# Experts of a routed feed-forward stage: part of the gate and up weights as plain float32, the output factors on other engines, and the split weights in another place of memory

## The chip, the cores and the metric

The kernel runs on one core of one Trainium2 chip. The metric is the device time of one execution in microseconds (us), as the median of several runs. Lower is better. Everything is float32 in memory, and the result has to agree with a float32 reference.

## What is computed

The reference is a network of two blocks. The first has dilated attention, gated scans and a gated linear recurrence in turn; the second has a hybrid mixer (pooling, a state space scan and a delta rule scan) and, at its end, a feed-forward stage of 16 experts in which each expert picks its own 128 tokens (16 experts, 1024 tokens, capacity factor 2). Cut to the part in question:

```python
def expert_choice_ffn(h, router_w, w_gate, w_up, w_down):
    ...
    gate, idx = lax.top_k(jnp.swapaxes(aff, 1, 2), cap)
    xe = jax.vmap(lambda hb, ib: hb[ib])(h, idx)
    hid = jax.nn.silu(jnp.einsum('becd,edf->becf', xe, w_gate)) * jnp.einsum('becd,edf->becf', xe, w_up)
    ye = jnp.einsum('becf,efd->becd', hid, w_down) * gate[..., None].astype(h.dtype)
    return jax.vmap(lambda ib, yb: jnp.zeros((T, D), yb.dtype).at[ib.reshape(-1)].add(yb.reshape(-1, D)))(idx, ye)
...
        x = x + m_lat[5][:, None] * expert_choice_ffn(h_lat, router_w[l], exp_w_gate[l], exp_w_up[l], exp_w_down[l])
...
    return rms_norm(x, final_norm_g)
```

The model's width is D = 1024 and an expert's width is 512, so the three weights of an expert are 1024x512, 1024x512 and 512x1024: 6.3 MB as float32, and 100 MB for all 16.

## The kernel before, in words

The program is one long list of instructions for each engine, put in order ahead of time by a scheduler from the way the code is written, its priorities and its buffers; on the chip each engine takes its list strictly in order and waits on semaphores. Everything up to the choice of tokens is the same list on every engine before and after the change. What concerns us is the last part, the function `experts` (from L2009), some 410 us of the span, and the pools that are laid out for it in `second_end` (L2206 to L2227).

**Products in three parts.** TensorE multiplies float32 data in the faster format float32r, which keeps fewer bits. To keep the accuracy, each operand is split into a high part (a cast to float32r, on ScalarE) and a low part (the difference, on VectorE or GpSimd). `mm3` (L135 to L141) then issues three matmuls into the same PSUM bank: high by high (L139), high by low of the moving operand (L140), low by high (L141). In the traces the stationary operand is the tokens (xeh, xel), and the moving operand is the weights (ehi, elo).

**Weights.** `units` (L2015 to L2029) brings one weight matrix in four units of 128x1024 float32 (512 KB). For each it issues one transfer on SP (SyncE, L2022) into a buffer `eraw` (27 of them, 14 in one pool and 13 in a second), the cast `ehi` on ScalarE (L2023) and the subtraction `elo`: on VectorE (L2025) for units 0 to 2 of each matrix, on GpSimd (L2027) for the fourth, and for all units of expert 0 on GpSimd. There are four buffers of ehi and four of elo. A unit holds two 128-row slices of gate or up (k = 0 to 7), or one of down.

**One expert.** `gather(e)` (L2031) turns the choice into indices and fetches the 128 chosen rows `xe` by an indirect transfer that GpSimd issues (L2047). `hidden(e)` (L2054) transposes xe on TensorE in two PSUM tiles of four chunks (L2061), splits them into xeh and xel (L132, L133), and computes gate and up (24 matmuls of 128x512 each) in the PSUM banks called `a`; then tanh on ScalarE (L2073) and two VectorE instructions (L2074, L2075) make `hid`. `down(e)` (L2078) transposes hid, splits it (hidh, hidl) and multiplies by down into the two banks called `o`, 24 more matmuls. VectorE reads each half from PSUM, multiplies it by the token's gate and by the row m5 (L2092), and GpSimd adds the result `ye` to the tokens' rows in memory with an indirect transfer (`accd`, L2094). Experts 14 and 15 aren't scattered: their part is added by matmuls at the end.

**Order.** The loop (L2128) asks in one step for gather(e+1), hidden(e) and down(e-1), so that an expert's gate and up lie beside the down product of the expert before. The scheduler mixes the instructions of both. SP's list is nothing but the weight transfers, each waiting for a free buffer; GpSimd's list mixes elo, xe and accd, and an instruction that waits holds up all that is behind it.

**Memory.** The split weights are in the pool `ew` (L2212) at the right (upper) end of memory, and the second pool of raw buffers, `er2`, next to it.

Of the kernel before, what the change touches and what calls it, by code (L numbers as in the profile page):

```python
# [10 lines left out]
F32 = mybir.dt.float32  # L11
F32R = mybir.dt.float32r
U32 = mybir.dt.uint32
AF = mybir.ActivationFunctionType
ALU = mybir.AluOpType
# [4 lines left out]
P = 128  # L20
# [7 lines left out]
def dap(ap, dims, off=0):  # L28

    return bass.AP(tensor=ap.tensor, offset=ap.offset + off, ap=[list(d) for d in dims])  # L30
# [1978 lines left out]
def experts(g, pool, rps, wp, vals, iota, place, m5, h2d, accd, finish):  # L2009


    nc, I = g.nc, g.I
    turns = cycle(rps)

    def units(blk, e, k, n):  # L2015
        out = []
        for u in range(4):
            rp, bufs = next(turns)
            raw = rp.tile([P, 1024], F32, name="eraw", tag="eraw", bufs=bufs)
            hi = wp.tile([P, 1024], F32R, name="ehi", tag="ehi", bufs=4)  # L2020
            lo = wp.tile([P, 1024], F32R, name="elo", tag="elo", bufs=4)
            nc.sync.dma_start(raw.rearrange("p (k n) -> p k n", n=n), blk[:, u * k:(u + 1) * k, :])  # L2022
            nc.scalar.copy(hi, raw)  # L2023
            if u < 3 and e > 0 or e == 15:
                nc.vector.tensor_sub(lo, raw, hi.bitcast(F32))  # L2025
            else:
                nc.gpsimd.tensor_tensor(lo, raw, hi.bitcast(F32), op=ALU.subtract)  # L2027
            out += [(hi[:, i * n:(i + 1) * n], lo[:, i * n:(i + 1) * n]) for i in range(k)]
        return out  # L2029

    def gather(e):  # L2031

        oh = pool.tile([P, 8, P], BF16, name="onehot", tag="onehot", bufs=1)
        nc.vector.tensor_tensor(oh, iota[:, None, 0:P].to_broadcast([P, 8, P]),
                                place[:, e, :, None].to_broadcast([P, 8, P]), op=ALU.is_equal)
        ps = g.psum("tr")
        for i in range(8):
            nc.tensor.matmul(ps[:, :5], oh[:, i], vals[:, i, e], start=i == 0, stop=i == 7)
        pk = pool.tile([P, 5], F32, name="picked", tag="picked", bufs=2)
        with g.up():  # L2040
            nc.vector.tensor_copy(pk, ps[:, :5])
        fi = pool.tile([P, 2], F32, name="fi", tag="fi", bufs=2)
        nc.vector.scalar_tensor_tensor(fi[:, 0:1], pk[:, 0:1], 128.0, pk[:, 1:2], op0=ALU.mult, op1=ALU.add)
        idx = pool.tile([P, 1], U32, name="idx", tag="idx", bufs=5)
        nc.vector.tensor_copy(idx, fi[:, 0:1])
        xe = pool.tile([P, D], F32, name="xe", tag="xe", bufs=2)
        nc.gpsimd.indirect_dma_start(out=xe, out_offset=None, in_=h2d, in_offset=bass.IndirectOffsetOnAxis(ap=idx, axis=0),  # L2047
                                     bounds_check=T - 1)
        nc.vector.tensor_add(fi[:, 1:2], pk[:, 2:3], pk[:, 3:4])
        gate = pool.tile([P, 1], F32, name="gate", tag="gate", bufs=5)  # L2050
        nc.vector.tensor_add(gate, fi[:, 1:2], pk[:, 4:5])
        return xe, idx, gate, fi[:, 0:1]

    def hidden(e, xe):  # L2054

        xh = pool.tile([P, 8, P], F32R, name="xeh", tag="xeh", bufs=2)
        xl = pool.tile([P, 8, P], F32R, name="xel", tag="xel", bufs=2)
        for c0 in range(0, 8, 4):
            tr = g.psum("tr")
            for i in range(4):  # L2060
                nc.tensor.transpose(tr[:, i * P:(i + 1) * P], xe[:, (c0 + i) * P:(c0 + i + 1) * P], g.ident)  # L2061
            with g.up():
                g.split(xh[:, c0:c0 + 4], xl[:, c0:c0 + 4], tr.rearrange("p (c t) -> p c t", t=P))
        sta = [(xh[:, k], xl[:, k]) for k in range(8)]
        wg = units(I["we_gate"][e], e, 2, 512)
        pg = g.psum("a")
        g.mm3(pg, sta, wg)
        wu = units(I["we_up"][e], e, 2, 512)
        pu = g.psum("a")
        g.mm3(pu, sta, wu)  # L2070
        hid = pool.tile([P, 512], F32, name="hid", tag="hid", bufs=2)
        with g.up():
            nc.scalar.activation(hid, pg, AF.Tanh, scale=0.5)  # L2073
            nc.vector.scalar_tensor_tensor(hid, hid, 1.0, pg, op0=ALU.add, op1=ALU.mult)  # L2074
            nc.vector.scalar_tensor_tensor(hid, hid, 0.5, pu, op0=ALU.mult, op1=ALU.mult)  # L2075
        return hid

    def down(e, hid, idx, gate, place):  # L2078
        tr = g.psum("tr")
        for i in range(4):  # L2080
            nc.tensor.transpose(tr[:, i * P:(i + 1) * P], hid[:, i * P:(i + 1) * P], g.ident)
        hh = pool.tile([P, 4, P], F32R, name="hidh", tag="hidh", bufs=2)
        hl = pool.tile([P, 4, P], F32R, name="hidl", tag="hidl", bufs=2)
        with g.up():
            g.split(hh, hl, tr.rearrange("p (c t) -> p c t", t=P))
        wd = units(I["we_down"][e], e, 1, 1024)
        y = pool.tile([P, D], F32, name="ye", tag="ye", bufs=2)
        for half in range(2):
            hs = slice(half * 512, (half + 1) * 512)
            pd = g.psum("o")  # L2090
            g.mm3(pd, [(hh[:, k], hl[:, k]) for k in range(4)], [(h[:, hs], l[:, hs]) for h, l in wd])
            nc.vector.scalar_tensor_tensor(y[:, hs], pd, gate, m5[:, hs], op0=ALU.mult, op1=ALU.mult)  # L2092
        if e < 14:
            nc.gpsimd.indirect_dma_start(out=accd, out_offset=bass.IndirectOffsetOnAxis(ap=idx, axis=0), in_=y,  # L2094
                                         in_offset=None, bounds_check=T - 1, compute_op=ALU.add)
            return

        oh = pool.tile([P, T], F32R, name="oht", tag="xeh", bufs=2)
        nc.vector.tensor_scalar(oh, iota, place, None, op0=ALU.is_equal)
        if e == 14:  # L2100
            yh, yl = (pool.tile([P, D], F32R, name=nm, tag="xel", bufs=2) for nm in ("yh", "yl"))
        else:
            yh, yl = (wp.tile([P, D], F32R, name=nm, tag=nm, bufs=4) for nm in ("ehi", "elo"))
        for half in range(2):
            hs = slice(half * 512, (half + 1) * 512)
            g.split(yh[:, hs], yl[:, hs], y[:, hs])
        ends.append((oh, yh, yl))
        if e == 14:
            return
        rp, bufs = rps[0]  # L2110
        acc = []
        for tok in range(8):
            acc.append(rp.tile([P, D], F32, name="acc", tag="eraw", bufs=bufs))
            nc.sync.dma_start(acc[-1], accd[tok * P:(tok + 1) * P])
        for tok in range(8):
            for half in range(2):
                hs = slice(half * 512, (half + 1) * 512)
                ps = g.psum("mm")
                for i, (oh, yh, yl) in enumerate(ends):
                    nc.tensor.matmul(ps, oh[:, tok * P:(tok + 1) * P], yh[:, hs], start=i == 0, stop=False)  # L2120
                    nc.tensor.matmul(ps, oh[:, tok * P:(tok + 1) * P], yl[:, hs], start=False, stop=i == 1)
                with g.up():
                    nc.vector.tensor_add(acc[tok][:, hs], acc[tok][:, hs], ps)
            finish(acc[tok], tok)

    ends = []
    at = {0: gather(0)}
    for e in range(17):  # L2128
        if e < 15:
            at[e + 1] = gather(e + 1)  # L2130
        if e < 16:
            hid = hidden(e, at[e][0])
        if e > 0:
            down(e - 1, prev, *at[e - 1][1:])
        prev = hid


def second_end(g, mix, mods, out, close, banks):

    nc, I, tc = g.nc, g.I, g.tc  # L2140
    h2d = g.dram.tile([T, D], F32, name="h2d")
    accd = g.dram.tile([T, D], F32, name="accd")
    with ExitStack() as es:
# [65 lines left out]
        m5, g3 = ev.tile([P, D], F32, name="m5"), ev.tile([P, D], F32, name="g3")  # L2209
        nc.sync.dma_start(m5, dap(mods, [[0, P], [1, D]], 5 * D))  # L2210
        nc.sync.dma_start(g3, dap(I["norm3"], [[0, P], [1, D]]))
        wp = es.enter_context(g.pool("ew", "right"))  # L2212
        rq = es.enter_context(g.pool("er2", "right"))
        with g.pool("ch") as cp:
            nc.vector.tensor_copy(place, choose(g, cp, aff, consts))
# [12 lines left out]
def body(g, out):  # L2228
# [101 lines left out]
    def banks():  # L2330
        pe.close()
        pe.enter_context(g.psum_pool("ps3", mm=2, a=2, o=2, tr=2))
    second_end(g, mix, mods, out, close, banks)
    pe.close()

# [120 lines left out]
```

## Time and profile before

| what | value |
|---|---|
| median of 3 runs | 3650.38 us (3646.48 to 3652.74) |
| the profiled execution's own time | 3659.12 us |
| its span, first to last instruction | 3656.9 us |
| mean granted TensorE clock | 0.935 |
| busy share: TensorE matmul, VectorE, ScalarE, GpSimd | 88%, 70%, 44%, 39% |
| first gate matmul of expert 0, from the span's start | 3246.85 us |
| ye of expert 0, of expert 14, of expert 15 begins | 3300.59, 3617.75, 3624.60 us |

The profile shows one execution. PE is TensorE, PEld its weight loads, DVE is VectorE, ACT is ScalarE, POOL is GpSimd, SP is SyncE, which issues transfers; a name with q (SPq) is the engine's own instruction queue. The profiled execution took 8.7 us more than the median of the runs, 0.24%. In what follows places are told in us from the start of the span.

### The profile page before, as it was taken

The numbers are of one execution on the slowest core, as the hardware profiler recorded it, in microseconds if no ns is written. First come the engines' busy times: TensorE is split into PE (matmuls) and PEld (weight loads), VectorE is DVE, ScalarE is ACT, GpSimd is POOL, SyncE is SP. The second block draws the span as 40 slices with busy tenths as digits, with TensorE's granted clock in tenths as the row PEclk, the third lists the DMA queues.
The fourth block names the chain that finished last, engine by engine and source line by source line (L and its number), as shares of the span: only waits on it lengthen the run. The fifth ranks groups of instructions, "written<-read, shape, count | busy, mean of one in ns | idle before, by whom it ended". The sixth has DMA issues, their size and how long they took to land.

```text
span 3656.9 us, 63623 instructions
## 1 busy us (share of the span) xinstructions
PE 3228.8 (88%) x23752; PEld 2610.4 (71%) x23752; DVE 2576.0 (70%) x5604; ACT 1595.0 (44%) x3332; POOL 1439.0 (39%) x1431
## 2 busy tenths in 40 slices
PE   7998898999979999999999989688896878858887
PEld 6887776766658787878787867566675766636665
DVE  4776664346675777976868686779994765678887
ACT  3444434544324545455545441344433331235665
POOL 4657773000041333433334321723214563345553
PEclk9999999999989999999999999789997888969999
DMA  5223244253242211111112135234337655768994
GB/s 181 82 87 102 87 140 137 74 177 99 96 153 73 70 64 53 58 54 40 56 45 76 54 126 174 77 82 133 104 108 187 140 135 205 211 219 295 312 332 148
DMA packets 374001, 461.28 MB, mean 126 GB/s; under 512 B 150419, under 2 KB 280723, under 8 KB 373692
## 3 DMA queue, kind: packets, MB, share of 16 engines
q1 hardware_dynamic: 359852, 407.93, 36.1%
q0 software_dynamic: 13840, 49.29, 4.4%
q8 instruction: 187, 3.06, 0.4%
q14 instruction: 122, 1.00, 0.1%
HBM read 357.57 MB, written 104.27 MB: 126 GB/s over the span
## 4 chain that ended last, share of the span: by engine, by line
PE 46%; DVE 23%; DMA 9%; issue 9%; POOL 8%; ACT 3%; SPq 2%; DVEq 0%; POOLq 0%; ACTq 0%
PE mm L139 9%; PE mm L140 9%; PE mm L141 9%; PE a L249 2%; POOL aw L966 2%; DVE cacc L1145 2%; DVE elo L2025 2%; DMA srow<-rdsl 1%; DMA aw<-in_ada_w_dram 1%; PE a L406 1%; PE o L225 1%; POOL wlo L116 1%; DVE gtmp L1465 1%; PE a L141 1%; DVE u_kb L187 1%
## 5 line engine op out<-in xcount | busy, mean ns | idle before, releaser
L116 POOL TENSOR_TENSOR wlo<-wraw,whi 128x1024 fp32r<-128x1024 f32 (+1 forms) x131 | 328.2, 2509 | 528.1 <-ACT whi L115 517.7
L2023 ACT CAST ehi<-eraw 128x1024 fp32r<-128x1024 f32 x192 | 200.4, 1050 | 144.5 <-PE a L141 100.7
L139 PE MATMUL mm<-x1h,whi 128*128 128x512 f32 x576 | 235.4, 409 | 3.3 <-DVE G L921 1.7
L140 PE MATMUL mm<-x1l,whi 128*128 128x512 f32 x576 | 233.9, 406 | 1.8 <-DVE x1l L133 1.8
L141 PE MATMUL mm<-x1h,wlo 128*128 128x512 f32 x576 | 233.8, 406 | 0.0
L139 PE MATMUL mm<-whi,x1h 128*128 128x256 f32 x768 | 221.8, 289 | 0.4 <-DVE G L921 0.4
L2025 DVE TENSOR_TENSOR elo<-eraw,ehi 128x1024 fp32r<-128x1024 f32 x138 | 196.8, 1460 | 35.7 <-ACT ehi L2023 34.2
L141 PE MATMUL mm<-whi,x1l 128*128 128x256 f32 x768 | 219.6, 286 | 0.0
L140 PE MATMUL mm<-wlo,x1h 128*128 128x256 f32 x768 | 219.1, 286 | 0.0
L115 ACT CAST whi<-wraw 128x1024 fp32r<-128x1024 f32 (+1 forms) x131 | 136.0, 1040 | 158.0 <-PE mm L140 78.5
L2027 POOL TENSOR_TENSOR elo<-eraw,ehi 128x1024 fp32r<-128x1024 f32 x54 | 138.9, 2577 | 161.9 <-ACT ehi L2023 144.1
L140 PE MATMUL mm<-wlo,xh 128*128 128x256 f32 x640 | 185.5, 290 | 1.9 <-POOL wlo L116 1.9
L141 PE MATMUL mm<-whi,xl 128*128 128x256 f32 x640 | 185.5, 290 | 0.0
L139 PE MATMUL mm<-whi,xh 128*128 128x256 f32 x640 | 184.8, 290 | 0.0
L139 PE MATMUL mm<-x2h,whi 128*128 128x512 f32 x400 | 168.2, 420 | 10.2 <-ACT cu L1134 5.7
L139 PE MATMUL mm<-whi,yin 128*128 128x512 f32 x352 | 150.2, 430 | 23.4 <-DVE z L824 14.1
L141 PE MATMUL mm<-x2h,wlo 128*128 128x512 f32 x400 | 164.9, 413 | 0.8 <-POOL wlo L116 0.8
L140 PE MATMUL mm<-x2l,whi 128*128 128x512 f32 x400 | 164.9, 412 | 0.0
L966 POOL TENSOR_SCALAR aw<-aw,ac 128x128 f32<-128x128 f32 x256 | 123.7, 498 | 85.5 <-DMA aw<-in_ada_w_dram 51.9
L139 PE MATMUL mm<-xh,whi 128*128 128x512 f32 x336 | 137.6, 410 | 20.0 <-ACT whi L115 16.7
L139 PEld LDWEIGHTS mm<-whi,x1h 128*128 128x128 f32 x768 | 146.8, 191 | 3.1 <-issue 1.0
L140 PEld LDWEIGHTS mm<-wlo,x1h 128*128 128x128 f32 x768 | 146.8, 191 | 0.6
(742 smaller groups left out, 10437.4 us busy)
## 6 DMA issues: line engine op xcount, KB each, us to landing
eraw<-in_we_gate_dram SPq DMA_DIRECT2D x64, 512.0 KB
eraw<-in_we_up_dram SPq DMA_DIRECT2D x64, 512.0 KB
eraw<-in_we_down_dram SPq DMA_DIRECT2D x64, 512.0 KB
yin<-yd POOLq DMA_DIRECT2D x29, 1024.0 KB, 9.7
aw<-in_ada_w_dram SPq DMA_DIRECT2D x96, 256.0 KB
yd<-y_hl SPq DMA_DIRECT2D x80, 256.0 KB
wraw<-in_w_dram SPq DMA_DIRECT2D x25, 512.0 KB
wraw<-in_w_out_dram SPq DMA_DIRECT2D x24, 512.0 KB
```

Of the source, the lines that this page charges most:

```text
L115: nc.scalar.copy(hi[:, :sz], raw[:, :sz])
L116: nc.gpsimd.tensor_tensor(lo[:, :sz], raw[:, :sz], hi[:, :sz].bitcast(F32), op=ALU.subtract)
L139: nc.tensor.matmul(ps, sh, mh, start=first and i == 0, stop=False)
L140: nc.tensor.matmul(ps, sh, ml, start=False, stop=False)
L141: nc.tensor.matmul(ps, sl, mh, start=False, stop=last and i == n - 1)
L187: nc.vector.tensor_sub(c32(kb), bc[:, :, il:il + 1].to_broadcast([P, nck, 32]), bc)
L249: nc.tensor.matmul(ap[32 * c:32 * c + 32, o + lo:o + hi], sta[:, o + 32 * c:o + 32 * c + 32], mov[:, o + lo:o + hi], start=True, stop=True)
L966: nc.gpsimd.tensor_scalar(w[:, k], w[:, k], at(k), 0.0, op0=ALU.mult, op1=ALU.add)
L1145: nc.vector.scalar_tensor_tensor(acc, u[:, i:i + n], cw[:, i:i + 1], acc, op0=ALU.mult, op1=ALU.add)
L2023: nc.scalar.copy(hi, raw)
L2025: nc.vector.tensor_sub(lo, raw, hi.bitcast(F32))
L2027: nc.gpsimd.tensor_tensor(lo, raw, hi.bitcast(F32), op=ALU.subtract)
```

## The change

It does three things, in `experts` and its pools.

1. `units` has a new argument `plain`. Gate and up are called with plain=1: their fourth unit (k = 6 and 7) stays as it arrived, with no ehi and no elo. A new helper `product` does the first six slices by `mm3` and the last two with one ordinary float32 matmul each. For these, the last two of the eight chunks of the transposed tokens are copied as float32 (`xew`, by ScalarE), and xeh and xel are made for six chunks, so that the second half of each is 128x256 now.
2. For experts 0 to 13 ScalarE reads each half of the down product from PSUM and multiplies it by the gate; GpSimd then multiplies the whole 128x1024 tile by m5, ahead of the indirect transfer accd. Experts 14 and 15 keep the VectorE instruction.
3. The pool `ew` moves to the lower end of memory, above the tiles m5 and g3; `er2` takes its place at the upper end.

```diff
-    def units(blk, e, k, n):
+    def units(blk, e, k, n, plain=0):
+
         out = []
         for u in range(4):
             rp, bufs = next(turns)
             raw = rp.tile([P, 1024], F32, name="eraw", tag="eraw", bufs=bufs)
+            nc.sync.dma_start(raw.rearrange("p (k n) -> p k n", n=n), blk[:, u * k:(u + 1) * k, :])
+            if u >= 4 - plain:
+                out += [raw[:, i * n:(i + 1) * n] for i in range(k)]
+                continue
             hi = wp.tile([P, 1024], F32R, name="ehi", tag="ehi", bufs=4)
             lo = wp.tile([P, 1024], F32R, name="elo", tag="elo", bufs=4)
-            nc.sync.dma_start(raw.rearrange("p (k n) -> p k n", n=n), blk[:, u * k:(u + 1) * k, :])
             nc.scalar.copy(hi, raw)
...
+    def product(ps, sta, mov):
+
+        whole = [i for i, m in enumerate(mov) if not isinstance(m, tuple)]
+        parts = [i for i, m in enumerate(mov) if isinstance(m, tuple)]
+        g.mm3(ps, [sta[i] for i in parts], [mov[i] for i in parts], last=False)
+        for i in whole:
+            nc.tensor.matmul(ps, sta[i], mov[i], start=False, stop=i == whole[-1])
...
+        xw = pool.tile([P, 2, P], F32, name="xew", tag="xew", bufs=2)
...
+            t3 = tr.rearrange("p (c t) -> p c t", t=P)
+            m = min(4, 6 - c0)
             with g.up():
-                g.split(xh[:, c0:c0 + 4], xl[:, c0:c0 + 4], tr.rearrange("p (c t) -> p c t", t=P))
-        sta = [(xh[:, k], xl[:, k]) for k in range(8)]
-        wg = units(I["we_gate"][e], e, 2, 512)
+                g.split(xh[:, c0:c0 + m], xl[:, c0:c0 + m], t3[:, :m])
+                if c0 == 4:
+                    nc.scalar.copy(xw, t3[:, 2:4])
+        sta = [(xh[:, k], xl[:, k]) for k in range(6)] + [xw[:, k] for k in range(2)]
+        wg = units(I["we_gate"][e], e, 2, 512, 1)
         pg = g.psum("a")
-        g.mm3(pg, sta, wg)
-        wu = units(I["we_up"][e], e, 2, 512)
+        product(pg, sta, wg)
+        wu = units(I["we_up"][e], e, 2, 512, 1)
         pu = g.psum("a")
-        g.mm3(pu, sta, wu)
+        product(pu, sta, wu)
...
-            nc.vector.scalar_tensor_tensor(y[:, hs], pd, gate, m5[:, hs], op0=ALU.mult, op1=ALU.mult)
+            if e < 14:
+                nc.scalar.activation(y[:, hs], pd, AF.Copy, scale=gate)
+            else:
+                nc.vector.scalar_tensor_tensor(y[:, hs], pd, gate, m5[:, hs], op0=ALU.mult, op1=ALU.mult)
         if e < 14:
+            nc.gpsimd.tensor_tensor(y, y, m5, op=ALU.mult)
             nc.gpsimd.indirect_dma_start(out=accd, out_offset=bass.IndirectOffsetOnAxis(ap=idx, axis=0), in_=y,
...
-        wp = es.enter_context(g.pool("ew", "right"))
+        wp = es.enter_context(g.pool("ew"))
```

The scheduler makes a new order from this. Three places of it follow. In the rows the number is the instruction's line (lines of the changed file are some 4 to 18 higher), and "x3" means three alike behind each other.

GpSimd's list in the middle of the experts, about two experts of it, before:

```order
L2047 DMA xe<-h2d,idx 128x1024
L2027 TENSOR_TENSOR elo<-eraw,ehi 128x1024 x3
L2094 DMA accd<-ye,idx 1024x1024
L2047 DMA xe<-h2d,idx 128x1024
L2027 TENSOR_TENSOR elo<-eraw,ehi 128x1024 x3
L2094 DMA accd<-ye,idx 1024x1024
```

and now:

```order
L2114 TENSOR_TENSOR ye<-ye,m_33798 128x1024
L2115 DMA accd<-ye,idx 1024x1024
L2059 DMA xe<-h2d,idx 128x1024
L2031 TENSOR_TENSOR elo<-eraw,ehi 128x1024
L2114 TENSOR_TENSOR ye<-ye,m_33798 128x1024
L2115 DMA accd<-ye,idx 1024x1024
L2059 DMA xe<-h2d,idx 128x1024
L2031 TENSOR_TENSOR elo<-eraw,ehi 128x1024
```

Of the three subtractions of an expert one is left, that of down's fourth unit, and the multiplication by m5 stands new ahead of accd; xe and the subtraction stand behind both.

VectorE's list around an expert's ye, before:

```order
L133 TENSOR_TENSOR hidl<-tr,hidh 128x512
L2043 SCALAR_TENSOR_TENSOR fi<-picked 128x1
L2049 TENSOR_TENSOR fi<-picked 128x1
L2092 SCALAR_TENSOR_TENSOR ye<-o,gate,m_33798 128x512 x2
L2051 TENSOR_TENSOR gate<-fi,picked 128x1
L2025 TENSOR_TENSOR elo<-eraw,ehi 128x1024 x3
L2045 CAST idx<-fi 128x1
L2074 SCALAR_TENSOR_TENSOR hid<-hid,a 128x512
L2025 TENSOR_TENSOR elo<-eraw,ehi 128x1024 x3
L133 TENSOR_TENSOR xel<-tr,xeh 128x512 x2
```

and the same place now:

```order
L2029 TENSOR_TENSOR elo<-eraw,ehi 128x1024 x2
L2057 CAST idx<-fi 128x1
L2063 TENSOR_TENSOR gate<-fi,picked 128x1
L2029 TENSOR_TENSOR elo<-eraw,ehi 128x1024
L2091 SCALAR_TENSOR_TENSOR hid<-hid,a 128x512
L133 TENSOR_TENSOR xel<-tr,xeh 128x512
L133 TENSOR_TENSOR xel<-tr,xeh 128x256
L2029 TENSOR_TENSOR elo<-eraw,ehi 128x1024 x2
```

The two ye instructions are gone from VectorE, the second xel is half as large, and the xel pair stands ahead of more of the subtractions.

ScalarE's list of one expert now (before, it held no ye, and twelve ehi to an expert):

```order
L2027 CAST ehi<-eraw 128x1024 x4
L132 CAST xeh<-tr 128x512
L2027 CAST ehi<-eraw 128x1024 x2
L132 CAST xeh<-tr 128x256
L2110 ACTIVATE ye<-o,gate 128x512 x2
L2027 CAST ehi<-eraw 128x1024 x2
L132 CAST hidh<-tr 128x512
L2080 COPY xew<-tr 128x256
L2027 CAST ehi<-eraw 128x1024 x3
L2090 ACTIVATE hid<-a 128x512
```

The two ye stand ahead of casts of the next units, so that these wait until the down product is done.

## Rows read from the trace of the kernel before

**Rows 1.** PE's waits, 3240:3657: who waited for whom, us in total, times, longest.

```profile
PE a L140 <- POOL elo L2027: 15.7, 4, 5.8
PE a L140 <- DVE elo L2025: 14.1, 8, 4.7
PE a L141 <- DVE xel L133: 11.9, 7, 3.2
PE o L140 <- DVE elo L2025: 4.6, 6, 2.5
```

**Rows 2.** DVE's timeline at ye of experts 0, 1, 5, 14: start, duration.

```profile
3300.59 0.75 DVE L2092 SCALAR_TENSOR_TENSOR ye<-o,gate,m 128x512 f32<-128x512 f32 x1 [0.47 <-PE o L141]
...
3321.47 0.74 DVE L2092 SCALAR_TENSOR_TENSOR ye<-o,gate,m 128x512 f32<-128x512 f32 x1
...
3423.47 0.74 DVE L2092 SCALAR_TENSOR_TENSOR ye<-o,gate,m 128x512 f32<-128x512 f32 x1
...
3617.75 0.73 DVE L2092 SCALAR_TENSOR_TENSOR ye<-o,gate,m 128x512 f32<-128x512 f32 x1
```

**Rows 3.** Windows: length, busy us per engine (instructions), PEclk, DMA share, GB/s.

```profile
3369.00:3396.00 27.00, 21.34 (x94) 16.22 (x94) 19.42 (x23) 14.67 (x17) 16.94 (x6) 0.87 0.85 279
...
3465.00:3487.00 22.00, 19.21 (x94) 14.64 (x93) 20.23 (x24) 14.44 (x16) 8.73 (x5) 1.00 0.96 364
```

**Rows 4.** PE's timeline after its three kinds of long waits: start, duration, [idle before].

```profile
3264.03 0.79 PE L140 MATMUL a<-elo,xeh 128*128 128x512 f32 x1 [4.73 <-DVE elo L2025]
...
3292.56 0.80 PE L140 MATMUL a<-elo,xeh 128*128 128x512 f32 x1 [4.04 <-DVE elo L2025]
...
3411.87 0.80 PE L140 MATMUL a<-elo,xeh 128*128 128x512 f32 x1 [5.83 <-POOL elo L2027]
```

**Rows 5.** POOL's timeline, experts 5 (three rows) and 9 (last row).

```profile
3400.05 4.71 POOL L2094 DMA_INDIRECT accd<-ye,idx  x1 [1.69 <-DVE gate L2051]
3405.06 4.38 POOL L2047 DMA_INDIRECT xe<-h2d,idx  x1 [0.30 <-issue]
3409.46 2.36 POOL L2027 TENSOR_TENSOR elo<-eraw,ehi 128x1024 fp32r<-128x1024 f32 x1
...
3508.26 1.59 POOL L2094 DMA_INDIRECT accd<-ye,idx  x1 [0.16 <-issue]
```

**Rows 6.** DVE's timeline at four places.

```profile
3258.78 6.33 DVE L2025 TENSOR_TENSOR elo<-eraw,ehi 128x1024 fp32r<-128x1024 f32 x2
...
3405.02 3.48 DVE L2025 TENSOR_TENSOR elo<-eraw,ehi 128x1024 fp32r<-128x1024 f32 x3
...
3501.06 4.82 DVE L2025 TENSOR_TENSOR elo<-eraw,ehi 128x1024 fp32r<-128x1024 f32 x3 [0.21 <-ACT ehi L2023]
3505.80 1.40 DVE L2092 SCALAR_TENSOR_TENSOR ye<-o,gate,m 128x512 f32<-128x512 f32 x2
```

**Rows 7.** PE's timeline: float32 matmuls (L1153) among float32r ones; transposes.

```profile
2434.24 1.88 PE L1153 MATMUL tr<-cu,blockones 128*128 128x512 f32 x4
2435.56 0.80 PE L141 MATMUL mm<-x2h,wlo 128*128 128x512 f32 x1
2436.19 0.39 PE L139 MATMUL mm<-x2h,whi 128*128 128x512 f32 x1
...
2445.79 0.39 PE L141 MATMUL mm<-x2h,wlo 128*128 128x512 f32 x1
...
3503.75 1.03 PE L2061 MATMUL tr<-ident,xe 128*128 128x128 f32 x8
```

**Rows 8.** Prices: lines by form in 3300:3600; L2223 (ns min/median/max).

```profile
L2073 ACT ACTIVATE hid<-a 128x512 f32<-128x512 f32 x13 | 7.8, 598 | 7.7 <-PE a L141 6.7 <-PE a L140 1.0
...
L2223 POOL TENSOR_TENSOR acc<-acc,g x3: 2351/2408/2421, 3636.0 to 3646.7; 128x1024 f32<-128x1024 f32 x3
```

**Rows 9.** SP's waits before a weight transfer, 3080:3657: us, times, longest.

```profile
SPq L2022 <- DVE elo L2025: 132.9, 89, 6.9
...
SPq L2022 <- DMA eraw<-in_we_gate_dram: 7.9, 8, 1.4
```

## The prediction

> **What bounds the kernel now.** Only the experts change, so I read that stage alone, from its first gate matmul at 3246.85 us. First the waits of PE, since PE's list is the longest there. It waits 15.7 us for a POOL elo (4 times), 14.1 and 4.6 us for DVE elos and 11.9 us for xel [rows 1]. The POOL elo waits stand in front of matmuls into `a`, that is gate and up. The reader is to see that PE doesn't lack weights: it lacks their low halves.
>
> Then the pace, from one ye to the next [rows 2]. Expert 0 to 1 took 20.9 us, experts 1 to 5 (3423.47 - 3321.47)/4 = 25.5 us each, experts 5 to 14 (3617.75 - 3423.47)/9 = 21.6 us each. PE's own work sets the floor: 42 rows of float32r matmuls from 2436.19 to 2445.79 give 9.60/41 = 0.234 us each, and eight transposes take 1.03 us [rows 7]. An expert has 72 such matmuls and 12 transposes: 16.8 + 1.55 = 18.4 us. So the early experts lose 7 us each and the later ones 3.2.
>
> Then why they lose it. Early: POOL's list is in order. Its accd took 4.71 us, its xe 4.38 and only then came the elo (2.36) for which PE had idled 5.83 us [rows 4, 5]. Later, accd took 1.59 [rows 5]. After such an idle stretch PE runs below full clock: the window of one early expert has a granted clock of 0.87, a later one 1.00 [rows 3]. As the lower level is half, 0.87 means that some 7 of the 27 us ran at half clock, which cost up to 3.5 us beside the wait. Right at the start DVE was held instead: two elos took 6.33 us at 3258.78 where three in a row take 3.48 elsewhere, with POOL elos beside them, and PE idled 4.73 and 4.04 us [rows 4, 6]. Later it is xel: two ye (1.40 us) stand ahead of it on DVE [rows 6].
>
> **The change, part by part.**
>
> *Float32 quarter on PE.* Each of gate and up loses 6 float32r matmuls and gets 2 float32 ones. In the trace four L1153 instructions, which are two such matmuls of the program, and one float32r matmul take from 2434.24 to 2436.19, 1.95 us; less 0.234 that is 0.86 us for each float32 matmul of 128x512 [rows 7]. Per k: 0.86 instead of 0.70; per expert 4 x 0.16 = +0.64 us, on PE, so on the path: new floor 60 x 0.234 + 4 x 0.86 + 1.55 = 19.0 us. The bounds are 0.70 (no cost) and, at half clock, twice 0.86. The Trainium skill (FP8 and Floating Point Precision, TensorE Precision Notes) says that true float32 makes four passes through the array; by that a k would cost 4 x 0.234 = 0.94 us, by an estimate, and the 16 experts 4 x 0.08 x 16 = 5 us more than by the row, on which the sum goes.
>
> *Subtractions and casts dropped.* Two of POOL's three elos per expert go (2.36 each), exactly those of gate's and up's fourth units. So the wait that costs most has nothing left to wait for: k = 6 and 7 need only the raw weights, which are there long before. SP mostly waits for buffers (132.9 us for DVE elos alone) and rarely for a landing (7.9 us, 8 times) [rows 9]. ACT loses two casts and DVE half of one xel, off the path.
>
> *ye.* DVE loses 1.40 us per expert [rows 6], ahead of xel. ACT gets two reads of PSUM, not seen before in this form: the nearest row is tanh on 128x512 from PSUM, 0.598 us [rows 8]; ACT was busy 14.4 of 22 us [rows 3], so this and the xew copy (at most the same 0.6) hide. POOL gets a 128x1024 product of two tiles: L2223 took 2.41 (2.35 to 2.42) [rows 8]. POOL still ends 2 x 2.36 - 2.4 = 2.3 us lighter. But two kinds of instruction exclude each other: three DVE elos at 3501.06 took 4.82 us rather than 3.48, beside one POOL elo [rows 6]. The new product would do to a DVE elo what each POOL elo did: up to 2.4 us a time, once, where two such meetings go. I count the balance as nothing. The Trainium skill (SBUF — State Buffer, the two separate sides) calls it an exclusive lock between GpSimd and a DVE instruction with two SBUF inputs; the trace agrees, with the 4.82.
>
> *New waits.* On ACT, ye waits for the last matmul of down, and the casts behind it wait too. They are of the next units, with four buffers of each half, so up to four units of about 1.4 us of PE are in hand. On POOL, the product, accd, xe and down's fourth elo now stand behind ye: 2.4 + 4.7 + 4.4 + 2.4 = 13.9 us at the early, slow prices, against some 17 from ye to the point where the next down product needs that elo (a pace of 20.8 less two thirds of down's 24 x 0.234 us). 3 us in hand.
>
> *Memory places.* Split weights and raw buffers change places; all earlier owners are done long before, as the first weights land well ahead of use. Zero; below a few us late at the start if not, once.
>
> **The sum.** Against the profiled execution's 3659.1.
> - Before ye of expert 0: the 4.73 and 4.04 us go, with POOL relieved of two of 12 elos there, and about 2.5 us at half clock behind each (as 3.5 us in the early window): -14, less 2 x 0.64 of float32 cost: -13. Bounds: -6 if one stall stays, -19.
> - Experts 1 to 5, four paces: from 25.5 to the floor 19.0 plus what remains of the late loss. That loss is 3.2 us, of which 1.4 is ye ahead of xel: 19.0 + 1.8 = 20.8. So 4 x 4.7 = -19.
> - Experts 5 to 14, nine paces: 21.6 to 20.8: -7.
> - Expert 0 to 1 was 20.9 already: 0. Expert 15 and the end: the order there is alike; 0 to -3.
> Sum: -40, with ends worked out below. So the profiled execution would be 3619, and as it stood 8.7 us above the median of the runs shown, the median 3650.4 - 40 = 3610. I take **3609**, with 1 us of the end's bound. Cross-check from the waits [rows 1]: the POOL and DVE elo waits and xel sum to 46 us; if a third stays, 31 us go, and half clock of some 3 us on each of seven early experts gives 21 more; less 16 x 0.64 = 10: -42.
>
> **How far it can go.** Best: all 14 paces at 19.0 (they took 317 us): -51, and -13 ahead: 3586. Least, if the mechanism holds at all: only the 15.7 us and four half-clock stretches of 2.5 go, less 10: -16, 3635.
>
> **Rivals.**
> 1. *Only the early stalls go.* In the later experts the window of 22 us moves 364 GB/s at a DMA share of 0.96 [rows 3]. An expert's 26.4 us at 279 GB/s is 7.4 MB, and a pace of 20.8 needs 354 GB/s: hardly below that. For it: the share. Against it: SP waits for buffers, not landings [rows 9]. Then later paces stay at 21.6 or, with the float32 cost, 22.2: -13 - 4 x 3.6 + 0 to 5 = -22 to -27, so 3623 to 3628; chance 0.2.
> 2. *POOL's list becomes the bound* (slower). If accd and xe, at 4.7 and 4.4, are held 3 us longer than now, by DVE elos as they were in [rows 5], the elo of down comes too late in each expert: a stall as the 5.83 us one, and some 2.4 at half clock: 19.0 + 8.2 = 27.2 a pace rather than 22.65 on the mean of 14: +64, less the first 13: +51, 3701. It decides when ye-to-elo passes 17 us. For it: it adds 2.4 us ahead of accd. Against: POOL holds less work in all. Chance 0.04.
> 3. *Nothing to measure*: the stall moves from POOL's elo to DVE's (14.1 us already [rows 1]), because DVE and POOL exclude each other over the product as over the elos: early paces of 24.5, later ones 22: -4 + 4 - 5, 3645; chance 0.05.
>
> **How the numbers follow.** The forecast, 3609, has 0.7, with its own range 3594 to 3623. Rival 1 has 0.2, rival 3 has 0.05, rival 2 has 0.04; the last 0.01 is for anything slower. The range for 8 in 10 leaves out the best end and the last two rivals and takes in rival 1: 3592 to 3632. A measurement tells about 0.2%, 7 us. Faster by more: 0.7 + 0.2 + 0.02 of rival 3 = 0.92; within: 0.03; slower: 0.05.
>
> **What would show it.** In the changed profile: PE waits for POOL elo in front of `a` gone; ye of expert 0 (now on ACT) near 3288, paces near 20.8 from the first, granted clock near 1.00 in all windows; float32 matmuls of two instructions, 0.86 us; xel waits shorter; accd behind a POOL product of 2.4 us. Wrong if PE waits at `o` for a POOL elo, if ACT's ye holds casts so that PE waits for ehi, if the early accd and xe still stop PE, or if SP shows long waits for landings and later paces stay over 21.6.

## The result, and the profile after

The changed kernel takes 3603.97 us in the median of 4 runs (3598.18 to 3608.20), the kernel before 3650.98 (4 runs): the ratio is 0.9877, with a 95% interval of 0.9858 to 0.9896, so 47 us less by the medians and 45 by the ratio. The forecast was 3609. The profiled execution took 3603.50 us, its span is 3601.4 us, and the mean granted clock rose from 0.935 in the profiled execution of before to 0.943.

Of the 55.5 us between the two spans 5 are not the change's: the first transposes of expert 0 begin at 3240.02 us here and at 3245.06 before, and up to there the orders are the same. They begin anywhere from 3236 to 3245 in the traces of this case, and at 3240.62 in that of a kernel whose lists in the stage are those of before (part 3 alone, below). So I compare the *stage*, from those transposes to the end of the span: 411.8 us before, 361.4 after, 50 less. The two windows (columns as in [rows 3]), first before, then after:

```profile
3245.06:3656.90 411.84, 342.95 (x1520) 262.87 (x1520) 332.07 (x360) 243.84 (x276) 209.99 (x97) 0.93 0.79 263
...
3240.02:3601.40 361.38, 332.95 (x1456) 240.73 (x1456) 282.62 (x330) 226.19 (x288) 156.15 (x81) 0.96 0.84 300
```

PE was idle for 68.9 us of the stage before and for 28.4 after, 40.5 less. The rise of the granted clock from 0.93 to 0.96 is worth some 15 us more, by an estimate from these two rounded values. Against it stand some 10 us for the float32 matmuls. That makes some 45 of the 50 us.

PE's waits in the changed kernel, 3240:3602 (who waited for whom, us in total, times, longest), the counterpart of [rows 1]:

```profile
PE a L139 <- ACT xeh L132: 6.8, 4, 1.9
PE tr L2074 <- DMA xe<-h2d,idx: 5.7, 1, 5.7
PE a L140 <- DVE elo L2029: 4.8, 4, 2.1
...
PE a L141 <- DVE xel L133: 1.1, 1, 1.1
...
PE o L140 <- POOL elo L2031: 0.2, 1, 0.2
```

No wait for a POOL elo is left in front of gate and up (15.7 us in [rows 1]); those for DVE elos fell from 18.7 to 4.8 and those for xel from 11.9 to 1.1. The 5.7 us for the first xe were there before too.

The starts of ye for experts 0, 1, 5 and 9 on ACT and of expert 14 on DVE, from the timelines of the changed kernel, as in [rows 2]:

```profile
3275.17 1.27 ACT L2110 ACTIVATE ye<-o,gate 128x512 f32<-128x512 f32 x2
...
3294.72 1.27 ACT L2110 ACTIVATE ye<-o,gate 128x512 f32<-128x512 f32 x2
...
3373.27 1.26 ACT L2110 ACTIVATE ye<-o,gate 128x512 f32<-128x512 f32 x2
...
3448.27 1.26 ACT L2110 ACTIVATE ye<-o,gate 128x512 f32<-128x512 f32 x2
...
3562.77 0.75 DVE L2112 SCALAR_TENSOR_TENSOR ye<-o,gate,m 128x512 f32<-128x512 f32 x1 [0.21 <-PE o L141]
```

From expert 0 to 9 a pace is (3448.27 - 3275.17)/9 = 19.2 us. From 9 to 14 it is 22.9: *slower* than the 22.4 of before (3617.75 against 3505.80 for expert 9). Three windows (columns as in [rows 3]) show the same:

```profile
3265.00:3287.00 22.00, 22.00 (x103) 15.79 (x102) 17.13 (x20) 15.11 (x19) 14.90 (x7) 1.00 0.93 321
...
3376.00:3398.00 22.00, 22.00 (x101) 16.21 (x100) 19.29 (x23) 15.82 (x20) 11.66 (x6) 1.00 1.03 389
...
3442.00:3464.00 22.00, 18.38 (x67) 12.72 (x65) 16.36 (x14) 11.73 (x16) 8.25 (x3) 0.84 1.00 380
```

In the first two PE is busy all 22 us at full clock. In the second DMA carries 389 GB/s, more than in either window of [rows 3]. In the third PE gets through 67 instructions rather than 101, with a granted clock of 0.84. What happens there, on PE's timeline of the changed kernel:

```profile
3448.48 1.04 PE L2074 MATMUL tr<-ident,xe 128*128 128x128 f32 x8
3451.00 0.50 PE L139 MATMUL a<-ehi,xeh 128*128 128x512 f32 x1 [1.48 <-ACT xeh L132]
...
3454.10 0.80 PE L140 MATMUL a<-elo,xeh 128*128 128x512 f32 x1 [2.14 <-DVE elo L2029]
...
3456.58 0.63 PE L139 MATMUL a<-ehi,xeh 128*128 128x512 f32 x1
```

on ACT's:

```profile
3448.27 1.26 ACT L2110 ACTIVATE ye<-o,gate 128x512 f32<-128x512 f32 x2
3449.42 1.04 ACT L2027 CAST ehi<-eraw 128x1024 fp32r<-128x1024 f32 x1
3450.35 0.87 ACT L132 CAST xeh<-tr 128x512 fp32r<-128x512 f32 x2
```

on DVE's, the first and the last of four subtractions behind each other (the two between them take 1.21 us each):

```profile
3445.66 2.82 DVE L2029 TENSOR_TENSOR elo<-eraw,ehi 128x1024 fp32r<-128x1024 f32 x1 [1.06 <-ACT ehi L2027]
...
3450.67 3.38 DVE L2029 TENSOR_TENSOR elo<-eraw,ehi 128x1024 fp32r<-128x1024 f32 x1
```

and on POOL's, beside the first of these a subtraction of its own, beside the last the new product:

```profile
3444.97 2.41 POOL L2031 TENSOR_TENSOR elo<-eraw,ehi 128x1024 fp32r<-128x1024 f32 x1
3449.61 3.36 POOL L2114 TENSOR_TENSOR ye<-ye,m 128x1024 f32<-128x1024 f32 x1 [2.23 <-ACT ye L2110]
```

At expert 9 and the three after it the list has the eight transposes behind all 24 down matmuls, so PE has nothing between. The list of before has the same place late in the loop, where its paces were 22.4. PE waits for xeh, which stands behind ye and a cast on ACT, then for an elo, which waits out the new product on POOL; after that it runs at half clock (0.63 us busy rather than 0.40) until 3459.

### The profile page after: what moved, and what is told of

Read it like the earlier page. It is cut to its first block, busy times and chain, and to the rows that moved or that the text cites. A ratio compares the mean times of both kernels' runs of the same rounds, so it can differ in the third digit from the quotient of the medians.

```text
span 3601.4 us, 63422 instructions
## 1 busy us (share of the span) xinstructions
PE 3217.0 (89%) x23688; PEld 2585.4 (72%) x23688; DVE 2527.6 (70%) x5574; ACT 1577.9 (44%) x3344; POOL 1383.2 (38%) x1415
## 3 DMA queue, kind: packets, MB, share of 16 engines
q1 hardware_dynamic: 359852, 407.93, 36.3%
## 4 chain that ended last, share of the span: by engine, by line
PE 49%; DVE 22%; DMA 9%; issue 8%; POOL 7%; ACT 3%; SPq 2%; DVEq 0%; POOLq 0%; ACTq 0%
PE mm L139 10%; PE mm L140 9%; PE mm L141 9%; POOL aw L966 2%; PE a L249 2%; DVE cacc L1145 2%; PE a L406 1%; PE a L2041 1%; DMA aw<-in_ada_w_dram 1%; DMA srow<-rdsl 1%; PE a L141 1%; PE a L140 1%; PE o L225 1%; PE a L139 1%; POOL wlo L116 1%
## 5 line engine op out<-in xcount | busy, mean ns | idle before, releaser
L2029 DVE TENSOR_TENSOR elo<-eraw,ehi 128x1024 fp32r<-128x1024 f32 x136 | 184.8, 1381 | 47.1 <-ACT ehi L2027 46.7
L2027 ACT CAST ehi<-eraw 128x1024 fp32r<-128x1024 f32 x160 | 165.5, 1051 | 99.6 <-PE a L141 35.9
L141 PEld LDWEIGHTS mm<-whi,x1l 128*128 128x128 f32 x768 | 146.8, 191 | 0.3
```

What stands on the lines that cost most here:

```text
L141: nc.tensor.matmul(ps, sl, mh, start=False, stop=last and i == n - 1)
```

## The experiments

For six of the kernels, one row of a view they share: the window 3300:3440, some six or seven experts (columns as in [rows 3]).

The kernel before:

```profile
3300.00:3440.00 140.00, 118.39 (x536) 91.33 (x535) 111.86 (x123) 84.77 (x93) 82.42 (x29) 0.93 0.90 294
```

Part 2 alone:

```profile
3300.00:3440.00 140.00, 118.30 (x545) 91.87 (x544) 129.43 (x118) 91.96 (x107) 88.10 (x36) 0.96 0.92 311
```

Part 2 alone without its product on POOL:

```profile
3300.00:3440.00 140.00, 128.12 (x606) 98.95 (x606) 130.46 (x129) 101.63 (x120) 74.52 (x33) 1.00 0.99 339
```

The subtractions of gate and up moved to DVE:

```profile
3300.00:3440.00 140.00, 133.69 (x648) 104.46 (x647) 140.00 (x170) 101.67 (x114) 51.54 (x22) 1.00 1.03 366
```

Part 1 alone:

```profile
3300.00:3440.00 140.00, 140.00 (x639) 103.24 (x638) 118.92 (x164) 92.16 (x109) 44.32 (x22) 1.00 1.03 382
```

The full change:

```profile
3300.00:3440.00 140.00, 139.42 (x647) 103.18 (x648) 126.33 (x151) 98.58 (x125) 66.17 (x29) 1.00 1.03 379
```

The number behind the window's length is PE's busy time, the fifth pair is POOL's, and the granted clock and the DMA share stand near the end. PE's busy time is 118 us in the two kernels where POOL's is over 80, and goes up to 140 where POOL's is 44; between them the order isn't strict (66 us of POOL beside 139 of PE in the full change, 52 beside 134 with the subtractions on DVE). Part 2 alone adds to POOL and gains PE nothing.

Times, ratios to the runs of before on the same chip, and stage lengths:

| kernel | median us | ratio, 95% interval | stage us |
|---|---|---|---|
| full change | 3603.97 | 0.9877 (0.9858 to 0.9896) | 361.4 |
| part 1 alone | 3601.67 | 0.9853 (0.9830 to 0.9876) | 363.7 |
| part 2 alone | 3662.41 | 1.0021 (1.0008 to 1.0034) | 422.2 |
| part 3 alone | 3653.70 | 0.9996 (0.9984 to 1.0008) | 411.5 |
| parts 1 and 2 | 3606.93 | 0.9872 (0.9855 to 0.9889) | 363.8 |
| subtractions to DVE | 3619.06 | 0.9903 (0.9871 to 0.9935) | 377.6 |
| part 2 without the product | 3629.74 | 0.9939 (0.9917 to 0.9960) | 384.9 |
| full change without the product | 3596.79 | 0.9861 (0.9835 to 0.9887) | 352.7 |
| part 1, gathered three ahead | 3590.17 | 0.9834 (0.9799 to 0.9870) | 347.0 |
| full change, gathered three ahead | 3591.48 | 0.9843 (0.9811 to 0.9874) | 351.5 |
| part 1, gathered ahead in steps | 3628.14 | 0.9941 (0.9921 to 0.9961) | 387.1 |

The scheduler writes new lists for nearly every edit, so a difference between two rows holds the new order as well. In the stage the lists are alike for the kernel before and part 3 alone, for the full change and parts 1 and 2, and, but for one matmul and the product itself, for the full change with and without the product. For part 1 no run separates the shorter work of POOL from the new order that came with it; what the traces show is which waits went.

**The parts by themselves.** Part 1 alone, from the full change:

```diff
-            if e < 14:
-                nc.scalar.activation(y[:, hs], pd, AF.Copy, scale=gate)
-            else:
-                nc.vector.scalar_tensor_tensor(y[:, hs], pd, gate, m5[:, hs], op0=ALU.mult, op1=ALU.mult)
+            nc.vector.scalar_tensor_tensor(y[:, hs], pd, gate, m5[:, hs], op0=ALU.mult, op1=ALU.mult)
         if e < 14:
-            nc.gpsimd.tensor_tensor(y, y, m5, op=ALU.mult)
...
-        wp = es.enter_context(g.pool("ew"))
+        wp = es.enter_context(g.pool("ew", "right"))
```

> Part 1 alone: the float32 quarter, with ye on VectorE and the split weights where they were. Theory (the gain comes from the two subtractions per expert that leave GpSimd's list): the early paces drop to about 20 us, no PE wait in front of gate or up for a GpSimd elo is left, and the xel waits of the later experts stay; some three quarters or more of the gain: 3605 to 3620 us. Rival (it takes the ye move as well, since accd and xe are held by VectorE's work): early paces stay over 23 us and the time is above 3630.

Measured: 3601.67 us, a little under the expected range, and all of the gain. The paces to expert 9 are 19.0 us on the mean (ye at 3276.43 and 3446.99), and no wait for a POOL elo is left. One thing came out otherwise than expected: the waits for xel didn't stay. PE has none in this trace, though ye is still on DVE.

Part 2 alone, on the kernel before:

```diff
-            nc.vector.scalar_tensor_tensor(y[:, hs], pd, gate, m5[:, hs], op0=ALU.mult, op1=ALU.mult)
+            if e < 14:
+                nc.scalar.activation(y[:, hs], pd, AF.Copy, scale=gate)
+            else:
+                nc.vector.scalar_tensor_tensor(y[:, hs], pd, gate, m5[:, hs], op0=ALU.mult, op1=ALU.mult)
         if e < 14:
+            nc.gpsimd.tensor_tensor(y, y, m5, op=ALU.mult)
```

> Part 2 alone: ye on ScalarE and GpSimd, all weights split as before. Theory: GpSimd's list gets 2.4 us more per expert on top of its three subtractions, so the early stalls in front of gate and up stay or grow: 3645 to 3690 us. Rival (the ye instructions on VectorE were what delayed xel and all else): xel waits go and the time falls by 10 us or more, below 3640.

Measured: 3662.41 us, slower by 0.2%, as the theory had it in size, but not in kind. PE's waits in this kernel, 3240:3665:

```profile
PE a L140 <- DVE elo L2025: 28.5, 12, 4.6
PE o L140 <- DVE elo L2025: 11.5, 8, 1.7
...
PE a L141 <- DVE xel L133: 3.3, 1, 3.3
...
PE o L140 <- POOL elo L2027: 0.2, 1, 0.2
```

The waits for a POOL elo are gone here too, since the scheduler made another list for POOL; in their place those for DVE elos rose from 18.7 to 40 us. The xel waits went from 11.9 to 3.3, as the rival said, but no time was gained by it.

Part 3 alone is the move of the pool `ew`, and parts 1 and 2 are the full change without it:

```diff
-        wp = es.enter_context(g.pool("ew", "right"))
+        wp = es.enter_context(g.pool("ew"))
```

> Part 3 alone: the split weights at the lower end of memory. Theory: the order on the engines is the same but for one transfer, so 3650 within 6 us. Rival (the place decides when the first weights can be split): first gate matmul several us earlier or later, and the end with it.

> Parts 1 and 2 without the move in memory. Theory: the move is worth nothing, so as the full change, 3604 within 6 us, with paces of 19.2 us up to expert 9. Rival: without the move the start of the experts is later by several us.

Measured: 3653.70 and 3606.93 us; the move is worth nothing either way. And with parts 1 and 2 no faster than part 1, the move of ye gives nothing on balance beside the float32 quarter.

**Why part 2 alone is slower: without its product on POOL.**

```diff
         if e < 14:
-            nc.gpsimd.tensor_tensor(y, y, m5, op=ALU.mult)
```

> Part 2 alone, without GpSimd's product by m5 (the output lacks the factor m5 for experts 0 to 13). Theory (that product holds up VectorE's subtractions, which made part 2 alone slower): PE's waits for a VectorE elo fall from 40 us to 20 or less and the time to 3625 to 3645. Rival (ScalarE's ye ahead of xeh and of the casts is what costs): the waits for elo and xeh stay and the time is at 3655 or more.

Measured: 3629.74 us. PE's waits for DVE elos, 3240:3665:

```profile
PE a L140 <- DVE elo L2025: 16.1, 8, 4.6
...
PE o L140 <- DVE elo L2025: 5.6, 4, 1.7
```

They fell from 40 to 21.7 us. So without the product the move of ye is worth 3653.33 - 3629.74 = 24 us, and with it 33 are lost again. How much of the 33 is the product itself isn't shown: the lists of PE, DVE, ACT and POOL all differ between the two, and the DVE subtractions are stretched little more with the product than without: 138 elos take 1.62 us on the mean rather than 1.57, 8 us in all.

**The same in the full change.** The same edit, on the full change:

> The full change without GpSimd's product by m5 (the output lacks the factor m5 for experts 0 to 13). Theory (with GpSimd's list short, PE is at its own floor of 19 us up to expert 9, so the product is hidden): 3598 to 3606 us, the paces to expert 9 at 19.2. Rival (the product still holds up VectorE and through it PE, as it did without the float32 quarter): 3590 or less.

Measured: 3596.79 us, just below what the theory had, and the interval overlaps that of the full change, so the medians don't settle what the product costs. The traces say more, since the lists are alike. The stage is 8.7 us shorter, where the two other pairs of like lists differ by 0.4 and 2.4 us. An elo on DVE takes 1.24 us on the mean rather than 1.38, and PE has no wait for a DVE elo left (4.8 us with the product). Up to expert 9 a pace is 18.8 rather than 19.2, 4 us in all; the other 6 come off between experts 9 and 14, with 1 us back at the end. So the product is nearly hidden early in the loop and not hidden late in it.

**Is it float32, or the work that stands in POOL's list?** The kernel before, with the fourth subtractions of gate and up on DVE; all weights are split.

```diff
-            if u < 3 and e > 0 or e == 15:
+            if (u < 3 or k == 2) and e > 0 or e == 15:
```

> The kernel before with the fourth subtraction of gate and up moved from GpSimd to VectorE; nothing is left out, all weights are split. Theory (what the float32 quarter gives is that GpSimd's list is shorter): the waits for a GpSimd elo go, but VectorE takes 2 x 1.2 us more per expert; part of the gain, 3615 to 3640 us. Rival 1 (the gain is in the work that goes away, not where it stands): no gain or a loss, 3645 to 3665. Rival 2 (float32 itself costs more than it saves): 3600 or less.

Measured: 3619.06 us, 34 of the 52 us of part 1. POOL's busy time in the shared window falls from 82 to 52 us, paces are 19.9 from expert 1 to 9, and DVE is busy 140.00 of 140 us: it is the bound in that window. The float32 quarter takes those subtractions away altogether: DVE falls to 118.92, PE is busy 140.00, and the pace is PE's own. From ye of expert 0 to that of expert 9 this is worth 7 us (177.5 with the subtractions on DVE, 170.6 in part 1 alone). More of the difference lies ahead of it, since this edit leaves all subtractions of expert 0 on POOL: from the first transposes to ye of expert 0 it takes 52.8 us, with PE waits of 4.3 and 4.8 us for DVE elos as before, and part 1 alone 36.3 without them. From expert 9 on part 1 alone is 9.5 us the slower.

**The late experts.** Part 1 alone with the gather earlier, so that the scheduler puts the transposes inside the products of the expert before up to the end (also four xe tiles, six of idx and gate, three of fi):

```diff
-    at = {0: gather(0)}
+    at = {0: gather(0), 1: gather(1), 2: gather(2)}
     for e in range(17):
-        if e < 15:
-            at[e + 1] = gather(e + 1)
+        if e < 13:
+            at[e + 3] = gather(e + 3)
...
-            experts(g, ep, [(rp, 14), (rq, 13)], wp, *vals, place, m5, h2d, accd, last)
+            experts(g, ep, [(rp, 14), (rq, 11)], wp, *vals, place, m5, h2d, accd, last)
```

> Part 1 alone, with the tokens gathered three experts ahead (four xe tiles, two raw buffers fewer), which keeps the transposes of the next expert inside the products of the one before up to the end. Theory (the late paces of 23 us come from the order: the eight transposes stand behind all 24 down matmuls, so PE has nothing to do while xeh and elo are made, and then runs at half clock): paces of 19 to 20 us from expert 9 to 14, 15 to 20 us off, 3580 to 3588 us. Rival (the transfers bound the late experts: DMA share 1.03 there): late paces stay at 22 to 24, the time stays at 3602 or rises with two buffers fewer.

Measured: 3590.17 us, the lowest median here. The window 3440:3540 of part 1 alone:

```profile
3440.00:3540.00 100.00, 90.81 (x372) 64.21 (x372) 68.04 (x86) 54.37 (x65) 27.35 (x13) 0.95 0.82 282
```

and of this kernel:

```profile
3440.00:3540.00 100.00, 100.00 (x435) 74.69 (x434) 81.36 (x96) 67.72 (x81) 24.37 (x12) 1.00 0.82 304
```

Paces of 19.4 and 17.0 from expert 9 to 11 rather than 23.0 and 25.4, with the same DMA share: transfers are not what slows the late experts. The next paces are 26.1, 23.7 and 7.9. They are no loss: PE is busy 26.1 and 23.1 us of the first two, the list has part of the last experts' gate and up matmuls there, and the three make 19.2 on the mean. From ye of expert 0 to that of expert 14 it takes 268.6 us rather than 287.2, which is the 15 to 20 us expected. The median fell by 11.5 us only; in the traces the stage is 16.7 us shorter and began 4.5 later.

The full change with the same edits:

> The full change with the tokens gathered three experts ahead. Theory: the late order is mended here too, 15 to 20 us off the 3604 of the change, 3583 to 3592 us, a few us behind the same with part 1 alone, because ye on ScalarE and GpSimd gives nothing. Rival: with the order mended, the relief of VectorE shows and this one is the faster by 5 us or more.

Measured: 3591.48 us, the same as without part 2 within the intervals. The relief of DVE doesn't show here either.

A gentler start, gathering one ahead at first and three from expert 3 on (part 1 alone, the same tiles):

```diff
-    at = {0: gather(0), 1: gather(1), 2: gather(2)}
+    at = {0: gather(0)}
     for e in range(17):
-        if e < 13:
-            at[e + 3] = gather(e + 3)
+        for nxt in range(len(at), min(16, e + 2 + (e > 0) + (e > 2))):
+            at[nxt] = gather(nxt)
```

> Part 1 alone, the tokens gathered one expert ahead at first, two from expert 1 on and three from expert 3 on (four xe tiles, two raw buffers fewer). Theory (what holds the late paces is where the order puts the transposes; the early gathers of the three-ahead version delay the start by some 4 us): all paces 19 to 20 us from expert 1 to 14, 3578 to 3588 us. Rival (with raw buffers fewer or transfers at their bound, late paces rise again): 3592 or more.

A miss: 3628.14 us. Paces are 21.5 to 25.6 from expert 1 to 11. The edit didn't do what it was meant to: in the new list the last transposes of an expert stand at the end of the down block again, now early in the loop too. PE's timeline of this kernel:

```profile
3345.68 0.53 PE L2074 MATMUL tr<-ident,xe 128*128 128x128 f32 x3
...
3346.98 0.71 PE L2074 MATMUL tr<-ident,xe 128*128 128x128 f32 x5
3348.80 0.50 PE L139 MATMUL a<-ehi,xeh 128*128 128x512 f32 x1 [1.12 <-ACT xeh L132]
...
3351.42 0.79 PE L140 MATMUL a<-elo,xeh 128*128 128x512 f32 x1 [1.65 <-DVE elo L2029]
...
3353.04 0.63 PE L140 MATMUL a<-elo,xeh 128*128 128x512 f32 x1
```

Three transposes stand behind 20 of the 24 down matmuls and five behind all, then PE waits for xeh and elo and runs at half clock, as in the late experts of the full change. The granted clock in 3300:3440 is 0.94, and the DMA share 0.97 against 1.03 in part 1 alone. So this run doesn't speak against the place of the transposes; it shows that an earlier gather doesn't settle that place, and that with the same tiles and buffers another list can cost some 38 us (3590.17 with the gather three ahead throughout).

## Why the prediction was right

It named the place and the mechanism, and the time came out 5 us under 3609. The sum was further off than that: the stage lost 50 us in the traces where the sum has 40. The first experts and the early paces gave more than was forecast, the late ones less, and the medians fell by 47. By its steps:

- *No PE wait for POOL elos at gate and up; float32 at 0.86 us.* Both as forecast. On PE's timeline of the changed kernel:

```profile
3441.51 1.88 PE L2041 MATMUL a<-eraw,xew 128*128 128x512 f32 x4
3442.82 0.79 PE L140 MATMUL o<-elo,hidh 128*128 128x512 f32 x1
3443.45 0.39 PE L141 MATMUL o<-ehi,hidl 128*128 128x512 f32 x1
```

Two float32 matmuls (four instructions) and one float32r take 1.94 us; less 0.234 and halved, 0.85 each. The estimate of 0.94 by the four passes of the Trainium skill (FP8 and Floating Point Precision, TensorE Precision Notes) is too high here.
- *The first experts: -13.* Measured from the first transposes to ye of expert 0: 55.5 to 35.2 us, -20. The two stalls went as said: PE is idle 10.7 us of that stretch before and not at all now. Some 3 us of the rest are order: before, 13 gate matmuls of expert 2 (0.234 us each) stood ahead of that ye, now none. And the clock gave back more than the 5 us that I had priced: the granted clock of the stretch is 0.84 before and 0.94 now, some 7 us by an estimate from these values.
- *Experts 1 to 5: -19.* Measured -23.5 (102.0 to 78.6 us), 19.6 a pace. I had left 1.8 us of loss in each pace; where the products of two experts overlap in the list, PE waits for next to nothing and the floor of 19.0 is nearly reached.
- *Experts 5 to 14: -7.* Measured -4.8, and of two kinds: 5 to 9 -7.3, 9 to 14 +2.5. The same 1.8 us of loss was too much for the first and too little for the second. The step that failed is to carry one loss per pace through an order that changes from expert to expert.
- *Expert 0 to 1: 0; the end: 0 to -3.* Measured -1.3 and -0.5.
- *ye: 1.4 us per late pace on the good side, the product on POOL nothing.* The xel waits did fall, but it didn't take the move of ye: part 2 alone leaves 3.3 of 11.9 us, part 1 alone none, with ye still on DVE. So the 1.4 us that ye ahead of xel was said to cost a later pace isn't borne out. The balance was indeed near nothing in the full change, as two terms that nearly cancel: the stage takes 363.7 us in part 1 alone, 352.7 with ye moved and no product, 361.4 with the product. In the kernel before it wasn't: 24 us gained and 33 lost, new lists included.
- *Rival 1*, transfers: a pace below 20.8, at 354 GB/s, was said to be hardly possible; 389 GB/s came. The 7.9 us of [rows 9] were the landings of gate alone, with up and down it was 16.7; now SP waits 68.2 us for landings (31.7, 19.8 and 16.7 for up, gate and down), and PE has no wait for one. One sign of being wrong did show: the paces from expert 9 to 14 are 22.9 on the mean, over 21.6, while SP waits for landings. The three-ahead kernel tells that the order is the reason, not the transfers.
- *Rival 2*: POOL's product, accd, xe and elo fit into the pace (POOL's timeline of the changed kernel, expert 5):

```profile
3374.61 2.42 POOL L2114 TENSOR_TENSOR ye<-ye,m 128x1024 f32<-128x1024 f32 x1 [4.26 <-ACT ye L2110]
3377.32 2.27 POOL L2115 DMA_INDIRECT accd<-ye,idx  x1 [0.28 <-POOL ye L2114]
3381.99 1.88 POOL L2059 DMA_INDIRECT xe<-h2d,idx  x1 [2.40 <-DVE gate L2063]
3386.84 2.50 POOL L2031 TENSOR_TENSOR elo<-eraw,ehi 128x1024 fp32r<-128x1024 f32 x1 [2.96 <-ACT ehi L2027]
```

accd and xe take 2.3 and 1.9 us, not the 4.7 and 4.4 of [rows 5], and in the whole stage never more than 2.4 and 3.0.
- *Rival 3*, the stall moving to DVE's elos, is what part 2 alone does.

## What to carry to other kernels

Look for the instruction that the busiest engine waits for and ask what stands ahead of it in its queue: here moving two subtractions of 2.4 us per expert off an engine that was busy 82 of 140 us was worth 34 us, the new order included, and dropping them altogether some 17 more, much of it in the first expert, though the busiest engine got more to do. Moving an instruction off a loaded engine onto one that excludes it may give back what it brought, so try the parts of a change alone, and see whether the lists stayed the same before you price a difference. And where a scheduler writes the list, look at the list late in the loop as well as early: its quality may change from one round to the next.

## What the runs showed of the hardware that I had not expected

The core moved 389 GB/s over 22 us with PE busy throughout, where the kernel before had 279 in an early expert; and the views then give a DMA share above 1, 1.03. Subtractions on DVE and products on POOL hold each other up in both directions, and took turns in the place followed here: the product at 3449.61 began while a DVE subtraction ran (3449.53 to 3450.75, not stretched) and took 3.36 us rather than 2.42, to 3452.97; the next DVE subtraction, at 3450.67, took 3.38 rather than 1.21, to 3454.05. Reading PSUM with a scale on ACT took 0.69 us for 128x512, against 0.60 for tanh [rows 8].
